# Attention values as one block product of seven instead of eight, with its sums made during the recurrent branch's output projection

## The chip, the core and the metric

The kernel runs on one core of a Trainium2 chip. Time is device microseconds of one execution on that core, the median of three runs. The profile is of one further execution, taken by the hardware profiler; its time was 864.52 us, of which 862.8 us lie between the first and the last instruction (the span).

## The reference

One layer of a hybrid encoder: 512 tokens, width 1024, float32. What the change touches is the third column block of the input projection, the values v, which the attention then weighs.

```python
xn = rmsnorm(h, norm_mix_g[l])
u = jnp.einsum('bsd,de->bse', xn, w_in[l])
q, k, v, xr, gr, ga, gb = jnp.split(u, splits, axis=-1)
ya = chunked_band_attention(q, k, v, rel_table[l]) @ w_attn_out[l]
...
yb = (hr * jax.nn.gelu(gr)) @ w_rnn_out[l]
...
# in chunked_band_attention, 16 heads of 64, chunks of 64 tokens, band of 9 chunks
p = jax.nn.softmax(s, axis=-1).astype(v.dtype)
o = jnp.einsum('bhnqk,bnkhd->bnqhd', p, vb)
```

So v is a product of 512 x 1024 tokens by 1024 x 1024 weights.

## The kernel before

All matrices are held in two parts: a high part rounded to the format fp32r and a low part, the rest. `split` (L80) makes them, the high part by a copy on ScalarE (ACT, L82), the low part by a subtraction on VectorE (DVE, L83). A product of two such values is three matmuls, high by high, high by low and low by high (`mm3`, L74; its matmuls are L76 to L78). TensorE (PE) writes them into PSUM, of which there are eight banks of 512 columns: four with the tag mm, two s, two t.

The stages in order: the normalized tokens are turned into `xnT` (feature rows by token columns, 8 blocks k of 128 features); the recurrent branch's projections (xr, gr and the gates); q and k of head pair 0; value unit 0; yb, the recurrent branch's output projection, in eight tiles of 24 matmuls, with the scores of head 0 ahead of its seventh tile; q and k of pair 1; value unit 1; the scores of head 1; then 16 heads. Each head turns its probabilities with PE (`transposed`), fills in a q or k tile of a later pair, makes the scores of the head two further on, and weighs the values (`weigh`, L973). After them ya, wo and the feed-forward layer. The latter already makes its products of weight and token blocks by seven products for eight (`block_product`).

A value unit (`v_unit`, L890) makes two of the four groups of 256 value columns (0 and 3, then 1 and 2) for all tokens: four token tiles, 8 k, three matmuls of 512 columns each, 96 in all, into four mm banks. The result is split from PSUM into v.

Weights come through a plan of chunks (`plan`, `prefetch` L311, `weights` L339): each chunk is loaded from DRAM by the SP queue into one of three raw buffers of 512 KB (tag raw), and split into one of four buffers of both parts (tag whl), one chunk ahead of the work that uses it. A raw buffer is free for the next load once it is split; a whl buffer once its last matmul has read it.

The order on each engine is set by a scheduler that lists instructions as the code's order and its own estimates have it, except in stretches under `manual_schedule`, where the named engines follow the order of the code. PE does so in the heads. Engines run their queues in order, and wait for each other by semaphores.

## Time and profile before

| what | value |
|---|---|
| time, median of 3 runs | 864.15 us (863.87 to 864.16) |
| time of the profiled execution | 864.52 us |
| its span | 862.8 us |
| PE busy | 853.1 us, 99% of the span, 4938 matmuls |
| DVE busy | 601.8 us, 70% |
| ACT busy | 497.5 us, 58% |
| POOL (GpSimd) busy | 95.9 us, 11% |
| moved by DMA | 96.38 MB, mean 112 GB/s |
| value unit 0 on PE | from 185.3 us |
| yb on PE | from 208.0 us |
| value unit 1 on PE | 262.8 to 284.6 us |

A row of a group names the line, the engine, the operation, the tile written and the tiles read, the shapes and the count; then busy time and the mean of one in ns; then how long the engine was idle just before these instructions and what ended it. A window's row has the busy time of PE, PEld (weight loads into the array), DVE, ACT and POOL, each with its count of instructions, then the granted clock of TensorE as a share, the busy share of the DMA engines and GB/s. A matmul's duration in the trace overlaps the next one's; the pace is the distance from start to start.

### The profile page before, as it was taken

The page shows a single profiled execution, that of the slowest core. Times are in us where ns is not written, and L with a number is a line of the kernel's source. Part 1 is how long each engine was busy: PE and PEld are TensorE (multiplying, and loading weights), DVE is VectorE, ACT ScalarE, POOL GpSimd, SP SyncE. Part 2 cuts the span into 40 slices and gives each one's busy share as a digit, 9 for nine tenths or more (in the row PEclk, how much of TensorE's full clock was granted, in tenths as well). Part 3 has the DMA queues.
Part 4 walks back from the last instruction along what each step waited for, and adds up shares of the span by engine and source line. Part 5 has one row for each costly group of instructions (what it writes and reads, how often), then busy time and mean ns, then how long its engine had stood idle before and what let it go on. Part 6 is the DMA issues. An engine that isn't in the chain of part 4 may idle for free.

```text
span 862.8 us, 13012 instructions
## 1 busy us (share of the span) xinstructions
PE 853.1 (99%) x4938; PEld 750.9 (87%) x4938; DVE 601.8 (70%) x950; ACT 497.5 (58%) x878; POOL 95.9 (11%) x161
## 2 busy tenths in 40 slices
PE   8999999999999999999999999999999999999997
PEld 6988888888888888888888889999999999888885
DVE  5567656664333788787556557987888888698885
ACT  6595847754123688787533357555655556545434
POOL 2412111120010233333000000000000001000000
PEclk9999999999999999999999999999999999999998
DMA  8233232433333233222233622424333332437542
GB/s 281 66 112 107 75 112 84 123 97 98 98 110 96 76 98 108 77 81 68 74 98 119 247 67 69 135 91 131 98 99 98 98 99 94 139 103 233 178 134 98
DMA packets 88895, 96.38 MB, mean 112 GB/s; under 512 B 5912, under 2 KB 75120, under 8 KB 88832
## 3 DMA queue, kind: packets, MB, share of 16 engines
q1 hardware_dynamic: 87200, 92.03, 34.7%
q10 hardware_dynamic: 1232, 2.95, 0.9%
q8 instruction: 39, 0.64, 0.3%
q0 software_dynamic: 400, 0.57, 0.2%
q14 instruction: 24, 0.20, 0.1%
HBM read 93.39 MB, written 2.14 MB: 111 GB/s over the span
## 4 chain that ended last, share of the span: by engine, by line
PE 97%; DVE 1%; ACT 1%; DMA 0%; issue 0%; ACTq 0%; DVEq 0%
PE po_out L76 2%; PE po_out L78 2%; PE po_out L77 2%; PE o L973 2%; PE p_fu L78 2%; PE p_fg L78 2%; PE p_fg L77 2%; PE p_fg L76 2%; PE p_fu L76 2%; PE p_fu L77 2%; PE pT L953 2%; PE po_gb L76 2%; PE po_xr L77 2%; PE po_xr L76 2%; PE po_ga L78 2%; PE po_k L76 2%
## 5 line engine op out<-in xcount | busy, mean ns | idle before, releaser
L942 POOL TENSOR_SCALAR p<-p,rl 128x128 f32<-128x128 f32 (+3 forms) x61 | 37.6, 636 | 91.1 <-DVE rl L938 85.9
L936 DVE CUSTOM_DVE_ANT_0 p<-s,bias 128x128 f32<-128x128 f32 (+2 forms) x64 | 28.7, 486 | 12.1 <-PE s L928 9.9
L937 ACT ACTIVATE p<-p,m 128x128 f32<-128x128 f32 (+2 forms) x64 | 35.6, 557 | 2.5 <-DVE m L936 2.2
L1158 POOL TENSOR_TENSOR act_lo<-act,act_hi 128x1024 fp32r<-128x1024 f32 x1 | 2.4, 2412 | 304.6 <-ACT act_hi L1157 304.6
L83 DVE TENSOR_TENSOR whl_qk<-raw_qk,whl_qk 128x1024 fp32r<-128x1024 f32 x16 | 20.3, 1270 | 18.5 <-ACT whl_qk L82 18.1
L76 PE MATMUL po_out<-whl_fo,act_hi 128*128 128x512 f32 (+1 forms) x80 | 30.8, 385 | 0.5 <-ACT c_u L373 0.5
L78 PE MATMUL po_out<-whl_fo,act_lo 128*128 128x512 f32 (+1 forms) x80 | 30.7, 384 | 0.0
L77 PE MATMUL po_out<-whl_fo,act_hi 128*128 128x512 f32 (+1 forms) x80 | 30.7, 384 | 0.0
L82 ACT ACTIVATE whl_qk<-raw_qk 128x1024 fp32r<-128x1024 f32 x16 | 16.9, 1055 | 20.5 <-PE po_v L78 9.8
L83 DVE TENSOR_TENSOR whl_fu_s<-s_fu,whl_fu_s 128x1024 fp32r<-128x1024 f32 x20 | 24.1, 1222 | 6.2 <-ACT whl_fu_s L82 6.2
L83 DVE TENSOR_TENSOR pp<-pT,pp 128x384 fp32r<-128x384 f32 (+1 forms) x48 | 26.9, 595 | 2.1 <-ACT pp L82 1.8
L77 PE MATMUL po_xr<-xnT,whl_xr 128*128 128x512 f32 (+1 forms) x80 | 27.7, 353 | 0.0
L77 PE MATMUL po_gr<-xnT,whl_gr 128*128 128x512 f32 (+1 forms) x80 | 27.5, 347 | 0.0
L78 PE MATMUL po_gr<-xnT,whl_gr 128*128 128x512 f32 (+1 forms) x80 | 27.3, 347 | 0.0
L78 PE MATMUL po_xr<-xnT,whl_xr 128*128 128x512 f32 (+1 forms) x80 | 27.2, 346 | 0.0
L76 PE MATMUL po_gr<-xnT,whl_gr 128*128 128x512 f32 (+1 forms) x80 | 27.1, 347 | 0.0
L83 DVE TENSOR_TENSOR whl_fg_s<-s_fg,whl_fg_s 128x1024 fp32r<-128x1024 f32 x20 | 24.0, 1223 | 4.1 <-ACT whl_fg_s L82 4.0
L76 PE MATMUL po_xr<-xnT,whl_xr 128*128 128x512 f32 (+1 forms) x80 | 26.3, 351 | 0.4 <-ACT xnT L569 0.4
L76 PE MATMUL po_k<-xnT,whl_qk 128*128 128x512 f32 x64 | 25.5, 398 | 0.0
L76 PE MATMUL po_q<-xnT,whl_qk 128*128 128x512 f32 x64 | 25.5, 398 | 0.0
L76 PE MATMUL po_ga<-xnT,whl_ga 128*128 128x512 f32 x64 | 25.4, 397 | 0.0
L76 PE MATMUL po_gb<-xnT,whl_gb 128*128 128x512 f32 x64 | 25.2, 394 | 0.0
(487 smaller groups left out, 3207.3 us busy)
## 6 DMA issues: line engine op xcount, KB each, us to landing
raw_fg<-in_w_ffn_in_dram SPq DMA_DIRECT2D x24, 512.0 KB, 4.2
raw_fu<-in_w_ffn_in_dram SPq DMA_DIRECT2D x22, 512.0 KB, 3.7
raw_qk<-in_w_in_dram SPq DMA_DIRECT2D x32, 256.0 KB, 3.1
raw_fo<-in_w_ffn_out_dram SPq DMA_DIRECT2D x16, 512.0 KB, 3.4
raw_xr<-in_w_in_dram SPq DMA_DIRECT2D x8, 512.0 KB, 3.5
raw_gr<-in_w_in_dram SPq DMA_DIRECT2D x8, 512.0 KB, 4.1
raw_ga<-in_w_in_dram SPq DMA_DIRECT2D x8, 512.0 KB, 4.1
raw_gb<-in_w_in_dram SPq DMA_DIRECT2D x8, 512.0 KB, 3.5
```

The source lines that it names most:

```text
L76: pe.matmul(o, sh, mh, start=start, stop=False, skip_group_check=parts)
L77: pe.matmul(o, sh, ml, start=False, stop=False, skip_group_check=parts)
L78: pe.matmul(o, sl, mh, start=False, stop=stop, skip_group_check=parts)
L82: act.activation(hi, src, AF.Copy)
L83: dve.tensor_sub(lo, src, f(hi))
L936: dve.tensor_tensor_reduce(prob[qb][:], scs[qb][:, 0:w], bias[:, S - w:S], -1.0, 3e38, ALU.add, ALU.min, nmax[:, qb:qb + 1])
L937: act.activation(prob[qb][:], prob[qb][:], AF.Exp, bias=nmax[:, qb:qb + 1], scale=-1.0, accum_out=lsum[:, qb:qb + 1])
L942: eng.tensor_scalar(prob[qb][:], prob[qb][:], rl[:, qb:qb + 1], 1.0, ALU.mult, ALU.mult)
L953: pe.transpose(pt[:, at * P:(at + 1) * P], prob[qb][:, kb * P:(kb + 1) * P], ident[:])
L973: pe.matmul(po[:, S - n:S], st, pp[i][:, part, lo:lo + n], start=kb == 0 and part == 0, stop=kb == NT - 1 and part == 1)
L1158: (dve if i else pool).tensor_sub(lo[:], o[:], f(hi[:]))
```

## The change

The tokens are cut into two halves of 256 and the features into two halves of 512, which gives blocks x11, x12, x21, x22 (token half, feature half); the value weights into w11, w12, w21, w22 (feature half, column side: groups 0 and 3, or 1 and 2). With

- s1 = x21 + x22, s2 = s1 - x11, s3 = x11 - x21, s4 = x12 - s2 (made by `x_sums`, each from both parts of the blocks),
- t1 = w12 - w11, t2 = w22 - t1 (`v_weight_sums`), t3 = t2 - w11, t4 = w21 - t2 (`v_weights`),

the seven products are x11 w11, s1 t1, s2 t2, s4 w22, s3 t3, x12 w21 and x22 t4. Each is two token tiles x 4 k x 3 = 24 matmuls of 512 columns. They accumulate in three pairs of banks, x and z (mm) and y (t). Copies on ACT keep an intermediate state of a bank (`keep`), adds on DVE join it with another bank, and the sums are split into v (`summed`, `given`).

The token sums s1 to s4 and the weight sums t1 and t2 are written in the code ahead of and inside yb. q and k of pair 1 go ahead of yb, and the scores of heads 0 and 1 lie inside it, ahead of its fifth and seventh tile. The seven products come after yb, directly ahead of head 0, and PE has them in the order of the code. The value weights are loaded in 14 buffers of 512 KB where there were 8: w11 comes three times, w22 twice, w12 and w21 once, each in two halves of its k, in 28 transfers of 256 KB for 16.

On PE 24 matmuls are fewer; from head 1 on the order of PE, DVE, ACT and POOL is as before. Three places where rows moved follow.

DVE during yb, from its first tile on. In the names, zb is the gate tile that is multiplied by a tile of yb out of PSUM, whl_yb the low part of yb's weights; before:

```order
L999 SCALAR_TENSOR_TENSOR zb0_456<-zb0_456,po_yb0_1858 128x512
L83 TENSOR_TENSOR whl_yb4_0_1921<-raw_yb4_0_1922,whl_yb4_0_1921 128x1024
L999 SCALAR_TENSOR_TENSOR zb0_456<-zb0_456,po_yb1_1894 128x512
L83 TENSOR_TENSOR whl_yb4_4_1926<-raw_yb4_4_1927,whl_yb4_4_1926 128x1024
L999 SCALAR_TENSOR_TENSOR zb2_457<-zb2_457,po_yb2_1920 128x512
L83 TENSOR_TENSOR whl_yb6_0_1983<-raw_yb6_0_1984,whl_yb6_0_1983 128x1024
L999 SCALAR_TENSOR_TENSOR zb2_457<-zb2_457,po_yb3_1956 128x512
L83 TENSOR_TENSOR whl_yb6_4_1988<-raw_yb6_4_1989,whl_yb6_4_1988 128x1024
L999 SCALAR_TENSOR_TENSOR zb4_458<-zb4_458,po_yb4_1982 128x512
```

and now, from the low part of s1 on (v_s1 is the buffer in which s1, s2 and s4 are made in turn, v_s1l and v_s2l are low parts, v_t1 and v_t2 the weight sums of the first half of the k blocks):

```order
L83 TENSOR_TENSOR v_s1l_1793<-v_s1_1787,v_s1h_1792 128x1024
L83 TENSOR_TENSOR whl_yb4_0_1870<-raw_yb4_0_1871,whl_yb4_0_1870 128x1024
L932 TENSOR_TENSOR v_s1_1787<-v_s1_1787,xnT_155 128x1024
L1105 SCALAR_TENSOR_TENSOR zb0_456<-zb0_456,po_yb1_1843 128x512
L83 TENSOR_TENSOR whl_yb4_4_1875<-raw_yb4_4_1876,whl_yb4_4_1875 128x1024
L934 TENSOR_TENSOR v_s1_1787<-v_s1_1787,xnT_155 128x1024
L322 TENSOR_TENSOR v_t1_0_1939<-raw_v_t_010_1933,raw_v_t_000_1930 128x1024
L1105 SCALAR_TENSOR_TENSOR zb2_457<-zb2_457,po_yb2_1869 128x512
L83 TENSOR_TENSOR v_s2l_1799<-v_s1_1787,v_s2h_1798 128x1024
L932 TENSOR_TENSOR v_s3_1788<-xnT_155 128x1024
L323 TENSOR_TENSOR v_t2_0_1940<-raw_v_t_110_1936,v_t1_0_1939 128x1024
L934 TENSOR_TENSOR v_s3_1788<-v_s3_1788,xnT_155 128x1024
```

Between the yb weights and zb rows stand token sums, weight sums and low parts.

DVE ahead of head 0. Before, the rows during value unit 1 (weights of later pairs, then the values out of PSUM):

```order
L83 TENSOR_TENSOR whl_qk2_0_2283<-raw_qk2_0_2284,whl_qk2_0_2283 128x1024
L83 TENSOR_TENSOR whl_qk2_4_2289<-raw_qk2_4_2290,whl_qk2_4_2289 128x1024
L83 TENSOR_TENSOR whl_qk3_0_2421<-raw_qk3_0_2422,whl_qk3_0_2421 128x1024
L83 TENSOR_TENSOR v1_2343<-po_v1_0_2219,v1_2343 128x2x128
L83 TENSOR_TENSOR v1_2343<-po_v1_1_2220,v1_2343 128x2x128
L83 TENSOR_TENSOR v2_0_2344<-po_v1_0_2219,v2_0_2344 128x2x128
L83 TENSOR_TENSOR v2_0_2344<-po_v1_1_2220,v2_0_2344 128x2x128
```

and now, during the products with t3 and w21:

```order
L337 TENSOR_TENSOR raw_v_t3_001_2280<-v_t2_1_2049,raw_v_t3_001_2280 128x1024
L83 TENSOR_TENSOR whl_v_t3_0_2272<-raw_v_t3_000_2274,whl_v_t3_0_2272 128x1024
L341 TENSOR_TENSOR v_t2_0_1940<-raw_v_w21_100_2323,v_t2_0_1940 128x1024
L83 TENSOR_TENSOR whl_v_t3_1_2273<-raw_v_t3_001_2280,whl_v_t3_1_2273 128x1024
L985 TENSOR_TENSOR v_keep0_2189<-v_z0_2157,v_keep0_2189 128x512
L341 TENSOR_TENSOR v_t2_1_2049<-raw_v_w21_101_2329,v_t2_1_2049 128x1024
L83 TENSOR_TENSOR whl_v_w21_0_2321<-raw_v_w21_100_2323,whl_v_w21_0_2321 128x1024
L985 TENSOR_TENSOR v_keep0_2189<-v_z1_2158,v_keep0_2189 128x512
L83 TENSOR_TENSOR v_big_2191<-v_keep0_2189,v_big_2191 128x2x128
L83 TENSOR_TENSOR v2_0_2312<-v_keep0_2189,v2_0_2312 128x2x128
L83 TENSOR_TENSOR whl_v_w21_1_2322<-raw_v_w21_101_2329,whl_v_w21_1_2322 128x1024
```

The sums of the weights stand between the low parts that they feed, and the values are split out of the kept sum in SBUF.

The SP queue ahead of head 0. Before, from the weights of value unit 1 on:

```order
L172 DMA raw_v1_0_0_2144<-in_w_in_dram 128x2x256 x2
L172 DMA raw_v1_0_2_2150<-in_w_in_dram 128x2x256 x2
L657 DMA bias2_2462<-ext_d_446 128x512
L172 DMA raw_v1_1_0_2224<-in_w_in_dram 128x2x256 x2
L172 DMA raw_v1_1_2_2230<-in_w_in_dram 128x2x256 x2
L172 DMA raw_qk2_0_2284<-in_w_in_dram 128x4x128 x2
L172 DMA raw_qk2_4_2290<-in_w_in_dram 128x4x128 x2
```

and now, from w11 on:

```order
L314 DMA raw_v_w11_000_2090<-in_w_in_dram 128x2x256 x2
L314 DMA raw_v_w11_001_2095<-in_w_in_dram 128x2x256 x2
L314 DMA raw_v_w22_110_2232<-in_w_in_dram 128x2x256 x2
L694 DMA bias3_2625<-ext_d_446 128x512
L314 DMA raw_v_w22_111_2237<-in_w_in_dram 128x2x256 x2
L314 DMA raw_v_t3_000_2274<-in_w_in_dram 128x2x256 x2
L314 DMA raw_v_t3_001_2280<-in_w_in_dram 128x2x256 x2
L314 DMA raw_v_w21_100_2323<-in_w_in_dram 128x2x256 x2
L314 DMA raw_v_w21_101_2329<-in_w_in_dram 128x2x256 x2
L169 DMA raw_qk2_0_2413<-in_w_in_dram 128x4x128 x2
L169 DMA raw_qk2_4_2419<-in_w_in_dram 128x4x128 x2
```

Each value load writes a raw buffer by two transfers (x2), and the loads of t3 and w21 stand between w22 and the weights of pair 2.

The diff, without the removed lines of `v_homes` and `v_unit`, which the listing above shows:

```diff
--- before.py
+++ after.py
@@ -109,16 +109,13 @@
 
     v_groups = ((0, 3), (1, 2))
 
-    def plan_v(u):
-        for kh in range(2):
-            plan(f"v{u}_{kh}", *(cols(w_in, C_V + gr * CW) for gr in v_groups[u]), rows=kh * S, kts=KT // 2)
-
+    v_kinds = ("w11", "t1", "t2", "w22", "t3", "w21", "t4")
     plan_qk(0)
-    plan_v(0)
+    plan_qk(1)
     for j in range(0, KT, 2):
         plan(f"yb{j}", cols(w_rnn_out, j * P))
-    plan_qk(1)
-    plan_v(1)
+    for kind in v_kinds:
+        plan(f"v_{kind}")
     for pr in range(2, HEADS // 2):
         plan_qk(pr)
     for j in (4, 6):
@@ -308,11 +305,51 @@
             return lambda part, k, at=every: hl[:, part, at]
         return lambda part, k, at=every: hl[:, part, k, at]
 
+    v_t1, v_t2 = [], []
+
+    def v_raw(kind, kh, half, u):
+        raw = wp.tile([P, 2, S], F32, tag="raw", bufs=3, name=f"raw_v_{kind}_{kh}{half}{u}")
+        at = kh * S + u * CW
+        for n, gr in enumerate(v_groups[half]):
+            sp.dma_start(out=raw[:, :, n * CW:(n + 1) * CW],
+                         in_=w_in[at:at + CW, C_V + gr * CW:C_V + (gr + 1) * CW].rearrange("(k p) e -> p k e", p=P))
+        return raw[:]
+
+    def v_weight_sums(u):
+
+        b11, b12, b22 = v_raw("t", 0, 0, u), v_raw("t", 0, 1, u), v_raw("t", 1, 1, u)
+        t1, t2 = (aw.tile([P, 2, S], F32, tag="v", bufs=4, name=f"v_t{n}_{u}")[:] for n in (1, 2))
+        dve.tensor_sub(t1, b12, b11)
+        dve.tensor_sub(t2, b22, t1)
+        v_t1.append(t1)
+        v_t2.append(t2)
+
+    def v_weights(kind):
+
+        hl = [wp.tile([P, 2, 2, S], F32R, tag="whl", bufs=4, name=f"whl_v_{kind}_{u}") for u in range(2)]
+        for u in range(2):
+            if kind == "t1":
+                src = v_t1[u]
+            elif kind in ("t2", "t4"):
+                src = v_t2[u]
+            elif kind == "t3":
+                src = v_raw(kind, 0, 0, u)
+                dve.tensor_sub(src, v_t2[u], src)
+            else:
+                src = v_raw(kind, int(kind[1]) - 1, int(kind[2]) - 1, u)
+                if kind == "w21":
+                    dve.tensor_sub(v_t2[u], src, v_t2[u])
+            split(hl[u][:, 0], hl[u][:, 1], src)
+        return lambda part, k: hl[k // 2][:, part, k % 2]
+
     def prefetch(n):
         while len(made) < min(n, len(chunks), index.get(barrier[0], len(chunks))):
             name, parts, rows, kts = chunks[len(made)]
             if name in strassen:
                 made.append(weight_sums(name))
+                continue
+            if name[:2] == "v_":
+                made.append(v_weights(name[2:]))
                 continue
             if not parts:
                 made.append(out_sums(name, rows))
@@ -468,7 +505,7 @@
     gm_p = ps.tile([P, S], F32, tag="s", bufs=2, name="gm_p")
     pe.transpose(gm_p[:, 0:8], gm_r[:], ident[0:8, 0:8])
     gm = cp.tile([P, 8], F32, name="gm")
-    _, xnT = features(xnp, "xn", "xnT")
+    xn_all, xnT = features(xnp, "xn", "xnT")
 
 
     vc = cp.tile([P, NV], F32, name="vc")
@@ -876,36 +913,101 @@
 
     vs = {}
 
...
+    def x_block(half, kh, part):
+        return xn_all[:, 4 * kh:4 * kh + 4, part, half * 256:half * 256 + 256]
+
+    def x_sums():
+
+        s, s3 = (zp.tile([P, 4, 256], F32, tag="late", bufs=2, name=f"v_s{n}")[:] for n in (1, 3))
+        out = {}
+
+        def parted(key, src):
+            pl, tag = (aw, "v") if key == "s4" else (aw2, "pt")
+            hi, lo = (pl.tile([P, 4, 256], F32R, tag=tag, bufs=4, name=f"v_{key}{n}") for n in "hl")
+            split(hi[:], lo[:], src)
+            out[key] = hi, lo
+
+        def chain(dst, first_, *rest):
+            (op, one, two) = first_
+            tc.keep_in_program_order(op(dst, one, two))
+            for op, one in rest:
+                op(dst, dst, one)
+
+        add, sub = dve.tensor_add, dve.tensor_sub
+        chain(s, (add, x_block(1, 0, 0), x_block(1, 1, 0)), (add, x_block(1, 0, 1)), (add, x_block(1, 1, 1)))
+        parted("s1", s)
+        chain(s, (sub, s, x_block(0, 0, 0)), (sub, x_block(0, 0, 1)))
+        parted("s2", s)
+        chain(s3, (sub, x_block(0, 0, 0), x_block(1, 0, 0)), (add, x_block(0, 0, 1)), (sub, x_block(1, 0, 1)))
+        chain(s, (sub, x_block(0, 1, 0), s), (add, x_block(0, 1, 1)))
+        return out, parted, s, s3
+
+    def v_pairs(gr, half):
+
         if gr in v_groups[0]:
...
+            o = aw.tile([P, 2, S], F32R, tag="v", bufs=4, name=f"v{gr}_{half}")[:]
+        elif gr == v_groups[1][0]:
+            o = v_big[0][:, half]
         else:
...
+            o = zp.tile([P, 2, S], F32R, tag="late", bufs=2, name=f"v{gr}_{half}")[:]
+        for t in range(2):
+            vs.setdefault(gr, {})[2 * half + t] = o[:, t].rearrange("p (a b d) -> p a b d", a=2, b=4)
+
+    v_big = []
+
+    def v_all(sums):
+        out, parted, s, s3 = sums
+        x_, y_ = ([mm_tile(f"v_{n}{a}", tag) for a in range(2)] for n, tag in (("x", "mm"), ("y", "t")))
+        z_ = [mm_tile(f"v_z{a}") for a in range(2)]
+
+        def product(banks, kind, rows, start):
+            w = weights(f"v_{kind}")
+            for a in range(2):
+                for k in range(4):
+                    if isinstance(rows, str):
+                        hi, lo = (o[:, k, a * P:(a + 1) * P] for o in out[rows])
+                    else:
+                        hi, lo = (x_block(*rows, part)[:, k, a * P:(a + 1) * P] for part in range(2))
+                    mm3(banks[a][:], hi, lo, w(0, k), w(1, k), start and k == 0, k == 3, parts=True)
+
+        def keep(o, banks):
+            for a in range(2):
+                act.activation(o[:, a], banks[a][:], AF.Copy)
+
+        def given(half, side, src):
+            for a in range(2):
+                for n, gr in enumerate(v_groups[side]):
+                    v = vs[gr][2 * half + a]
+                    split(v[:, :, 0::3], v[:, :, 1:3], src(a)[:, n * CW:(n + 1) * CW].rearrange("p (a b d) -> p a b d", a=2, b=2))
+
+        def summed(o, banks, half, side):
+            for a in range(2):
+                dve.tensor_add(o[:, a], banks[a][:], o[:, a])
+            for gr in v_groups[side]:
+                v_pairs(gr, half)
+            given(half, side, lambda a: o[:, a])
+
+        product(x_, "w11", (0, 0), True)
+        keeps = [rnp.tile([P, 2, 2, S], F32, tag="big", bufs=4, name=f"v_keep{n}") for n in range(2)]
+        v_big.append(rnp.tile([P, 2, 2, S], F32R, tag="big", bufs=4, name="v_big"))
+        x1, x2, z1 = keeps[0][:, 0], keeps[0][:, 1], keeps[1][:, 0]
+        keep(x1, x_)
+        product(z_, "t1", "s1", True)
+        keep(z1, z_)
+        parted("s4", s)
+        product(x_, "t2", "s2", False)
+        keep(x2, x_)
+        parted("s3", s3)
+        product(z_, "w22", "s4", False)
+        summed(x2, z_, 0, 1)
+        product(x_, "t3", "s3", False)
+        summed(z1, x_, 1, 1)
+        product(y_, "w21", (0, 1), True)
+        summed(x1, y_, 0, 0)
+        product(x_, "t4", (1, 1), False)
+        for gr in v_groups[0]:
+            v_pairs(gr, 1)
+        given(1, 0, lambda a: x_[a][:])
 
 
     def scores(h):
@@ -989,19 +1091,20 @@
             return gate(0, h - 8)
         (k_tile if h % 2 else q_tile)(2 + h // 2)
 
-    v_unit(0)
+    q_tile(1)
+    k_tile(1)
+    sums = x_sums()
     probs = {}
     for j in range(KT):
-        if j == 6:
-            probs[0] = scores(0)
+        if j in (4, 6):
+            probs[j // 2 - 2] = scores(j // 2 - 2)
         po = mm_tile(f"po_yb{j}")
         project(po, weights(f"yb{j - j % 2}"), j % 2, rnn)
+        if j in (3, 5):
+            v_weight_sums(j // 2 - 1)
         dve.scalar_tensor_tensor(zB[j], zB[j], 1.0, po[:], ALU.add, ALU.mult)
-    q_tile(1)
-    k_tile(1)
-    v_unit(1)
-    probs[1] = scores(1)
     with tc.manual_schedule(engines={mybir.EngineType.PE}):
+        v_all(sums)
         for h in range(HEADS):
             pp = transposed(h, probs.pop(h))
             fill(h)
```

More of the change, by code (lines that the diff above doesn't have):

```diff
@@ L877, in block_kernel @@
     vs = {}
-    def v_homes(gr):
+    def x_block(half, kh, part):
[21 more added lines that the diff above has]
+        return out, parted, s, s3
@@ L880, in v_homes @@
+    def v_pairs(gr, half):
         if gr in v_groups[0]:
-            return [aw.tile([P, 2, 4, HD], F32R, tag="v", bufs=8, name=f"v{gr}_{t}") for t in range(NT)]
-        if gr == v_groups[1][0]:
-            big = rnp.tile([P, 2, 2, S], F32R, tag="big", bufs=4, name=f"v{gr}")
-            rows = [big[:, t // 2, t % 2] for t in range(NT)]
-        else:
-            pairs = [zp.tile([P, 2, S], F32R, tag="late", bufs=2, name=f"v{gr}_{n}") for n in range(2)]
-            rows = [pairs[t // 2][:, t % 2] for t in range(NT)]
@@ L888, in v_homes @@
-        return [o.rearrange("p (a b d) -> p a b d", a=2, b=4) for o in rows]
-    def v_unit(u):
-        po = [mm_tile(f"po_v{u}_{t}") for t in range(NT)]
-        for kh in range(2):
-            wv = weights(f"v{u}_{kh}")
-            for kk in range(0, 4, 2):
-                for t in range(NT):
-                    toks = slice(t * P, (t + 1) * P)
-                    for k in (kk, kk + 1):
-                        xk = xnT[4 * kh + k]
-                        mm3(po[t][:], xk[:, 0, toks], xk[:, 1, toks], wv(0, k, every), wv(1, k, every),
-                            kh == k == 0, kh == 1 and k == 3)
-        homes = [v_homes(gr) for gr in v_groups[u]]
-        for t in range(NT):
-            for n, gr in enumerate(v_groups[u]):
-                v = homes[n][t]
-                v = v[:] if gr in v_groups[0] else v
-                split(v[:, :, 0::3], v[:, :, 1:3],
-                      po[t][:, n * CW:(n + 1) * CW].rearrange("p (a b d) -> p a b d", a=2, b=2))
-                vs.setdefault(gr, []).append(v)
+            o = aw.tile([P, 2, S], F32R, tag="v", bufs=4, name=f"v{gr}_{half}")[:]
+        elif gr == v_groups[1][0]:
+            o = v_big[0][:, half]
+        else:
+            o = zp.tile([P, 2, S], F32R, tag="late", bufs=2, name=f"v{gr}_{half}")[:]
```

## The prediction

> **Bound.** I read the page's first part, then the waits of PE, the windows of the stages that the change touches, PE's timeline there, and the groups of DVE and ACT by form.
>
> ```profile
> PE 853.1 (99%) x4938; PEld 750.9 (87%) x4938; DVE 601.8 (70%) x950; ACT 497.5 (58%) x878; POOL 95.9 (11%) x161
> PE busy L399 <- DVE eps_t L405: 1.2, 1, 1.2
> PE pt_mix_0t L567 <- DVE xs_mix L547: 1.1, 2, 0.9
> PE po_out L76 <- ACT c_u L373: 0.5, 1, 0.5
> PE po_xr L76 <- ACT xnT L569: 0.4, 2, 0.2
> ```
>
> PE is busy 99% of the span. Its four waits add up to 3.2 us, and they belong to the start and to the switch to the output stage. None lies in yb, the values or the attention. In the windows below the columns are PE, PEld, DVE, ACT and POOL busy, then clock, DMA share and GB/s: first value unit, yb, heads 0 to 7, and the feed-forward stage, which is already done as seven products for eight.
>
> ```profile
> 185.30:207.10 21.80, 21.80 (x98) 18.04 (x97) 9.68 (x13) 8.75 (x14) 2.94 (x3) 1.00 0.39 120
> 208.00:251.90 43.90, 43.90 (x196) 36.40 (x195) 17.10 (x27) 12.31 (x20) 2.22 (x5) 1.00 0.30 90
> 284.60:360.00 75.40, 75.40 (x422) 66.06 (x421) 60.36 (x142) 59.14 (x138) 25.51 (x46) 1.00 0.30 85
> 520.00:740.00 220.00, 220.00 (x1835) 219.91 (x1834) 180.28 (x249) 133.20 (x239) 2.41 (x1) 1.00 0.32 100
> ```
>
> PE has no gap in any of them at full granted clock, so time there is the number of matmuls times their pace. DVE is idle for 61% of yb (17.10 of 43.90). In the feed-forward stage PE stays dense with DVE at 82% (180.28 of 220), in the heads at 80%.
>
> **Removed.** Each value unit is 4 token tiles x 8 k x 3 = 96 matmuls of 512 columns, 192 for two. The pace:
>
> ```profile
> 185.32 0.39 PE L76 MATMUL po_v<-whl_v,xnT 128*128 128x512 f32 x1
> 207.08 0.22 PE L927 MATMUL s<-kh,q 128*128 128x128 f32 x1
> ...
> 208.00 0.39 PE L76 MATMUL po_yb<-rnn,whl_yb 128*128 128x512 f32 x1
> ```
>
> 96 starts lie from the first of these to the second, so (207.08 - 185.32) / 96 = 0.2267 us per matmul (the 0.39 is a duration that overlaps the next). Seven products of 2 x 4 x 3 = 24 make 168. 24 matmuls fall away: 24 x 0.2267 = 5.44 us. All other PE work remains: the q and k tiles of pair 1 and the scores of head 1 only change places. The shapes of the new matmuls are those of the old, so I take the pace to 1%: 5.39 to 5.50.
> The Trainium skill (TensorE: Matmul & The Clock Gate, back-to-back issue gap) gives 215.7 ns for 512 columns on a warm array; the trace here has 226.7, so it does not agree. By that page the gain would be 5.18 us; I stay with the row.
>
> **Added.** These rows carry the prices (busy, mean ns).
>
> ```profile
> L83 DVE TENSOR_TENSOR whl_fu_s<-s_fu,whl_fu_s 128x1024 fp32r<-128x1024 f32 x20 | 24.1, 1222 | 6.2 <-ACT whl_fu_s L82 6.2
> L386 DVE TENSOR_TENSOR c_u<-q_fu,keepa_fu 128x512 f32<-128x512 f32 x10 | 6.9, 690 | 3.5 <-PE q_fu L78 2.8 <-ACT keepa_fu L373 0.7
> L999 DVE SCALAR_TENSOR_TENSOR zb<-zb,po_yb 128x512 f32<-128x512 f32 x8 | 5.5, 688 | 12.0 <-PE po_yb L78 12.0
> L864 DVE TENSOR_TENSOR kl<-po_k,kh 64x512 fp32r<-64x512 f32 x16 | 11.0, 687 | 1.4 <-ACT kh L863 1.0
> L83 DVE TENSOR_TENSOR v<-po_v,v 128x256 fp32r<-128x256 f32 x16 | 6.4, 421 | 3.3 <-ACT v L82 3.1
> L936 DVE CUSTOM_DVE_ANT_0 p<-s,bias 128x512 f32<-128x512 f32 x16 | 10.9, 682 | 0.0
> L936 DVE CUSTOM_DVE_ANT_0 p<-s,bias 128x384 f32<-128x384 f32 x16 | 8.8, 550 | 0.2
> L936 DVE CUSTOM_DVE_ANT_0 p<-s,bias 128x256 f32<-128x256 f32 x16 | 6.7, 420 | 0.0
> L936 DVE CUSTOM_DVE_ANT_0 p<-s,bias 128x128 f32<-128x128 f32 x16 | 4.7, 292 | 11.9 <-PE s L928 9.9 <-POOL p L942 1.8
> L936 DVE DVE_READ_ACCUMULATOR2_ANT m<- 128x1 f32 x64 | 5.2, 82 | 0.0
> L938 DVE RECIPROCAL rl<-l 128x4 f32<-128x4 f32 x16 | 2.8, 174 | 1.3 <-ACT p L937 1.3
> L82 ACT ACTIVATE whl_v<-raw_v 128x1024 fp32r<-128x1024 f32 x8 | 8.4, 1055 | 9.1 <-issue 6.6 <-PE po_yb L78 1.7 <-PE po_k L78 0.8
> L82 ACT ACTIVATE v<-po_v 128x256 fp32r<-128x256 f32 x16 | 5.7, 379 | 4.0 <-DVE v L83 2.4 <-PE po_v L78 1.5
> L852 ACT ACTIVATE q<-po_q 64x512 fp32r<-64x512 f32 x16 | 9.5, 594 | 14.0 <-PE po_q L78 12.8 <-DVE q L853 0.8
> ```
>
> No row of before has the sums of the token blocks, of four blocks in 1024 elements a row; the nearest is the first, an SBUF-with-SBUF operation of that size: 1.22 us, below by nothing (one element per lane and step in every such row), above by the 1.47 quoted further down. The new copies of a product (128x512, PSUM to SBUF on ACT) stand nearest to the q row: 0.59 us.
>
> Between the two PE rows 207.08 and 208.00 lie six of a head's eight score matmuls, 0.92 us; with the two of 384 columns, 2 x 384/512 x 0.2267 = 0.34, a head's scores take 1.26. yb now lasts 8 x 24 x 0.2267 + 2 x 1.26 = 46.0 us on PE. DVE in it: 25 rows of 1.22 (10 token sums, 2 low parts of sums, 4 weight sums, 5 low parts of yb weights, 2 of w11, the sum and low part with which t3 and t1 begin) = 30.6; seven zb rows 4.8; the score rows of two heads 2 x (0.29 + 0.42 + 0.55 + 0.68 + four short ones of 0.08) = 4.5; k of pair 1 1.4; reciprocals 0.3. Sum 41.6 of 46.0, 90%.
> In the seven products DVE has 18 rows of 1.22, 6 adds of 0.69, 12 splits of 0.42 and one zb: 31.9 of 38.1, 84%. ACT has there 15 x 1.06 + 6 x 0.59 + 12 x 0.38 = 24.0 of 38.1. So all fits under PE in amount; with no cover the 16 sums and low parts in yb alone would cost 19.6 us. Whether it fits in order I walked through by these durations.
>
> Loads first. Three raw buffers of 512 KB circulate, and each load waits for the split that frees its buffer. The issue rows (KB each, median us to landing) and the spread of a value load:
>
> ```profile
> raw_v<-in_w_in_dram SPq DMA_DIRECT2D x16, 256.0 KB, 3.1
> raw_yb<-in_w_rnn_out_dram SPq DMA_DIRECT2D x8, 512.0 KB, 3.5
> x<-in_x_dram SPq DMA_DIRECT2D x4, 512.0 KB, 6.4
> DMA to landing us min/median/max: 2.8/3.1/4.7
> ```
>
> Two transfers of 256 KB per buffer: 3.7 us from freed to landed. The 14 value buffers against 8 before add 3.1 MB over some 84 us, 37 GB/s on top of 90.
>
> The walk of yb (0 = its first matmul). The first k low part of pair 1 is done by 1.5, s1 by 8.0, its low part 10.4, the next yb weights (yb4) 14.7, needed at 23.0; s2 15.9; the first weight sum, whose last buffer lands at 15.3, 17.1; t2 of it 21.4; yb6 weights 23.8 and 29.4, needed at 35.1; scores of head 0 30.1; the second pair of weight sums 31.3 and 34.6 (its load lands at 33.1); scores of head 1 37.3; w11 39.7, needed at 46.0: 6 us ahead. Then DVE waits for the first t3 load until 43.4, and the first half of t1 is ready at 45.8, needed at 51.5.
>
> The walk of the products (0 = first of w11; starts at 5.44 each; the second weight half is needed 1.36 later). A half is freed 4.08 or 5.44 into its product and refilled for the second next. t1's second half is ready at 3.2 (needed 6.8); t2 6.4 and 8.4 (10.9, 12.2); w22 11.9 and 14.9 (16.3, 17.7); the second t3 load lands 15.6; t3 18.0 and 21.0 (21.8, 23.1); w21 24.1 and 26.8 (27.2, 28.6); t4 29.5 and 32.2 (32.6, 34.0). The copies and adds that free the banks all come a product earlier than the bank is written again. The smallest distance is 1.8 us, at the second halves of w21 and t4. So no PE wait.
>
> Into the heads: Head 0's turned probabilities are done on DVE 5.6 us after the products end; before, they were done 290.2 - 285.4 = 4.8 us after the transposes began:
>
> ```profile
> 285.45 0.93 PE L953 MATMUL pT<-ident,p 128*128 128x128 f32 x7
> 288.63 1.61 DVE L83 TENSOR_TENSOR pp<-pT,pp 128x512 fp32r<-128x512 f32 x3
> 293.63 1.38 PE L973 MATMUL o<-pp,v 128*128 128x512 f32 x8
> ```
>
> There o began 8.2 us after the transposes; now the same transposes, q tile and scores lie between and make it some 8 us again, and the last value rows are done after 6.0: 2 us to spare, and from there the order is the old one. (Three rows that sum to 1.79 take 1.61 here: DVE rows overlap by some 0.09, so my walk is on the slow side.)
>
> **Sum.** Span 862.8 - 5.4 = 857.4. The profiled execution took 864.5, 1.7 around its span and 0.4 above the median of the runs, 864.15. Against the median: 864.15 - 5.44 = 858.7 us, 858.3 to 859.3 if up to half a microsecond of waits is overlooked.
>
> **Rivals.**
> First, DVE's rows are longer than taken. Not all 1024-element rows last 1.22:
>
> ```profile
> L83 DVE TENSOR_TENSOR whl_ga<-raw_ga,whl_ga 128x1024 fp32r<-128x1024 f32 x8 | 11.7, 1474 | 2.4 <-ACT whl_ga L82 2.4
> 174.35 1.64 DVE L83 TENSOR_TENSOR whl_v<-raw_v,whl_v 128x1024 fp32r<-128x1024 f32 x1
> ```
>
> At 1.47 the 25 rows of yb cost 6.3 more; 2.0 go into the wait for t3's load, 4.3 arrive at t1's second half with 3.6 to spare: 0.7 us, and the 6 us of DVE waits in the products take the rest: 859.4. Against it: the long rows lie where POOL works, and POOL has only the scaling of two heads and four copies in yb, nothing in the products after their start.
> The Trainium skill (SBUF — State Buffer, who interferes with whom) says that a DVE instruction with two SBUF inputs blocks with a GpSimd instruction that reads SBUF, and the two rows agree with it. By that rule the sums here are of the exposed kind and the case above is the one to expect in part.
> Second, and slower, the same at 1.64. All 25 + 18 rows 0.42 longer: 10.5 - 2.0 against 3.6 is 4.9 us at t1; in the products 16 x 0.42 + 3.6 - 6.4 = 3.9 against 1.8 is 2.1 more. 7.0 us of waits eat the gain: 865.7; from a mean of about 1.65 the change is slower by over 0.2%. One row in the trace of before is that long, so a mean there is unlikely.
> Third, the loads decide. At the 6.4 us of the first x loads t3's second half would be 0.8 late, w21's halves 1.9 and 1.3: 4 us, 862.7, no change. At 4.7, the longest value load, 0.2. For it: three buffers and a chain of load, sum, split; against it: DMA is busy 30% to 39%.
> That the change doesn't do what it says is excluded: the built order has 24 matmuls fewer, and PE, DVE, ACT and POOL in the old order from head 1 on.
>
> **Numbers.** Forecast 0.74 (858.7), long rows 0.10 (859.4), loads 0.09 (to 862.7), slower 0.07 (865.7). A measurement tells 0.2% (1.7 us) from no change. Faster: forecast, long rows and half of the load case, 0.88; same 0.05; slower 0.07. The range 858.0 to 861.5 leaves out the slower case and the late half of the loads.
>
> **Signs.** Right: matmuls of the products at 0.227 us from start to start; no PE wait with v_x, v_z, v_y or po_yb; DVE near 90% in yb and 84% in the products; the heads as before, 5.4 us earlier. Wrong: PE waiting for the low part of t1, w21 or t4 (DVE), for a raw_v load, or in heads 0 to 2 for pp.

## The result, and the profile after

The median is 859.06 us (858.73 to 859.59, six executions) against 864.15 (863.87 to 864.43): 5.1 us less, ratio 0.9941 with a 95% interval of 0.9928 to 0.9954. The forecast was 858.7 us in a range of 858.0 to 861.5. The profiled execution took 859.59 us, its span is 857.8.

The page's first line and the waits of PE, after:

```profile
PE 848.7 (99%) x4914; PEld 746.7 (87%) x4914; DVE 636.4 (74%) x984; ACT 511.1 (60%) x894; POOL 97.0 (11%) x161
PE busy L436 <- DVE eps_t L442: 1.2, 1, 1.2
PE po_out L76 <- ACT c_u L410: 0.5, 1, 0.5
PE po_xr L76 <- ACT xnT L606: 0.4, 2, 0.2
PE pt_mix_0t L604 <- DVE xs_mix L584: 0.2, 1, 0.2
```

24 matmuls are gone, DVE has 34.6 us more work and ACT 13.6, and PE waits where it waited before: at the start and at the switch to the output stage. No wait names v_x, v_z, v_y, po_yb or a head. The windows of yb, the seven products and heads 0 to 7 (PE, PEld, DVE, ACT, POOL busy, then clock, DMA share, GB/s):

```profile
196.40:242.30 45.90, 45.90 (x208) 38.22 (x207) 37.82 (x52) 18.64 (x31) 6.71 (x12) 1.00 0.54 172
242.50:280.60 38.10, 38.10 (x169) 31.48 (x168) 30.71 (x40) 24.50 (x36) 0.00 (x0) 1.00 0.34 101
280.60:356.00 75.40, 75.40 (x419) 66.00 (x418) 60.38 (x136) 58.24 (x133) 23.54 (x42) 1.00 0.34 96
```

DVE's share of yb rose from 39% to 82%, and PE stays dense over it. PE's timeline at both ends of the products:

```profile
242.53 0.39 PE L76 MATMUL v_x<-whl_v_w,xnT 128*128 128x512 f32 x1
...
280.39 0.39 PE L78 MATMUL v_x<-whl_v_t,xnT 128*128 128x512 f32 x1
280.62 0.49 PE L1055 MATMUL pT<-ident,p 128*128 128x128 f32 x3
```

168 matmuls in 280.62 - 242.53 = 38.09 us are 0.2267 each, the pace of before. To see where 5.09 of the expected 5.44 us went, here are three marks on PE, the first q matmul, the first weighing of head 0 and the last matmul of all, in the timeline before (its mark in the middle, 293.63, stands in the prediction):

```profile
174.44 0.39 PE L76 MATMUL po_q<-xnT,whl_qk 128*128 128x512 f32 x1
...
856.09 0.28 PE L78 MATMUL po_last<-whl_fo,act_lo 128*128 128x256 f32 x1
```

and after:

```profile
174.67 0.39 PE L76 MATMUL po_q<-xnT,whl_qk 128*128 128x512 f32 x1
...
288.47 0.62 PE L1075 MATMUL o<-pp,v 128*128 128x512 f32 x2
...
850.91 0.28 PE L78 MATMUL po_last<-whl_fo,act_lo 128*128 128x256 f32 x1
```

The touched stretch fell from 119.19 to 113.80 us, by 5.39; the rest up to the last matmul is 562.46 and 562.44. The start came 0.23 later, and what follows the last matmul took 6.89 after 6.71.

### The profile page after: what moved, and what is told of

It reads as the page before. It is cut to its first block, busy times and chain, and to the rows that moved or that the text cites. A ratio compares the mean times of both kernels' runs of the same rounds, so it can differ in the third digit from the quotient of the medians.

```text
span 857.8 us, 13023 instructions
## 1 busy us (share of the span) xinstructions
PE 848.7 (99%) x4914; PEld 746.7 (87%) x4914; DVE 636.4 (74%) x984; ACT 511.1 (60%) x894; POOL 97.0 (11%) x161
## 4 chain that ended last, share of the span: by engine, by line
PE 97%; DVE 1%; DMA 1%; ACT 1%; issue 0%; ACTq 0%; SPq 0%; DVEq 0%
PE po_out L76 2%; PE po_out L78 2%; PE po_out L77 2%; PE o L1075 2%; PE p_fu L78 2%; PE p_fg L78 2%; PE p_fg L77 2%; PE p_fg L76 2%; PE p_fu L76 2%; PE p_fu L77 2%; PE pT L1055 2%; PE po_gb L76 2%; PE po_xr L77 2%; PE po_xr L76 2%; PE po_ga L78 2%; PE po_q L76 2%
## 5 line engine op out<-in xcount | busy, mean ns | idle before, releaser
L1039 ACT ACTIVATE p<-p,m 128x128 f32<-128x128 f32 (+1 forms) x64 | 35.5, 555 | 5.3 <-DVE m L1038 5.0
L1038 DVE CUSTOM_DVE_ANT_0 p<-s,bias 128x128 f32<-128x128 f32 (+1 forms) x64 | 28.6, 486 | 11.3 <-PE s L1030 9.2
L76 PE MATMUL po_ga<-xnT,whl_ga 128*128 128x512 f32 x64 | 25.4, 397 | 0.0
L78 PE MATMUL po_ga<-xnT,whl_ga 128*128 128x512 f32 x64 | 25.0, 391 | 0.1
L77 PE MATMUL po_ga<-xnT,whl_ga 128*128 128x512 f32 x64 | 25.0, 390 | 0.0
```

The costliest lines, as they stand in the source:

```text
L76: pe.matmul(o, sh, mh, start=start, stop=False, skip_group_check=parts)
L77: pe.matmul(o, sh, ml, start=False, stop=False, skip_group_check=parts)
L78: pe.matmul(o, sl, mh, start=False, stop=stop, skip_group_check=parts)
L1038: dve.tensor_tensor_reduce(prob[qb][:], scs[qb][:, 0:w], bias[:, S - w:S], -1.0, 3e38, ALU.add, ALU.min, nmax[:, qb:qb + 1])
L1039: act.activation(prob[qb][:], prob[qb][:], AF.Exp, bias=nmax[:, qb:qb + 1], scale=-1.0, accum_out=lsum[:, qb:qb + 1])
```

## Experiments

Where no word is said of it, the listed edit leaves what is computed as it was, up to rounding.

### The changed kernel again

No edit; five executions beside the kernel before.

> The changed kernel once more, beside the kernel before, in five rounds. It is to settle whether the change is worth the 24 matmuls (5.44 us) or the 5.09 us by which the two medians differ. Theory (the pace times the count, all else hidden): the stretch from the first yb matmul to the first transpose of head 0 is again 5.4 shorter than the same work before, the median 5.2 to 5.6 below that of the kernel before, and what differs from 5.44 lies outside the touched stretch, at the start or after the last matmul. Rival (some hidden waits of 0.3 to 0.4 in the products): the same 5.1, and a PE wait of 0.3 or more between the first yb matmul and head 2.

859.22 us (859.08 to 859.39) against 864.28 (864.21 to 864.48), ratio 0.9941 (0.9929 to 0.9954): again 5.06. In its trace the first q matmul starts at 174.28 and head 0 is weighed from 288.06, so the stretch lasts 113.78, 5.41 less than before, and PE has the first three waits of the list above and no other. The rival with hidden waits falls. Nearly all of the missing 0.35 us lies outside the stretch that was changed. Between profiles of one and the same kernel the start moved by 0.39 (174.67, 174.28); which part of the 0.35 belongs to the start and which to the end stays open, since the one profile of before is of an execution that took 864.52, above its own median.

### The order alone

Against the changed kernel, shortened:

```diff
-    for kind in v_kinds:
-        plan(f"v_{kind}")
+    plan_v(0)
+    plan_v(1)
...
-    sums = x_sums()
...
-        if j in (3, 5):
-            v_weight_sums(j // 2 - 1)
...
-        v_all(sums)
+        v_unit(0)
+        v_unit(1)
```

> The new order alone: q and k of pair 1 ahead of yb, both heads' scores inside yb, the values after yb with PE in the code's order, but the values still made as eight products (the two value units of the kernel before, 192 matmuls), with no sums. Theory (the gain is the count of matmuls): the same time as the kernel before, 864.15 within 0.5 us, that is some 5.1 to 5.6 above the changed kernel. Rival (the order gives part of the gain, because it takes waits or a slow start of head 0 away): 861 to 863.5. Rival (the order costs something that the seven products hide): above 865.

864.80 us (864.66 to 864.93), ratio 1.0006 (0.9997 to 1.0014). So the order brings nothing; by the medians it costs some 0.5, though the interval also holds no difference, and from there to the changed kernel, 24 matmuls fewer, are 5.58 us. Of the 0.5, its trace shows one new wait:

```profile
PE po_v L76 <- DVE v L83: 0.2, 1, 0.2
```

With the units side by side, the second needs the four banks that the first has just filled, and at the third of them waits for the splits out of it (one matmul there starts 0.33 us later than the pace). The seven products alternate between x, z and y and have no such place.

### The cover taken away

```diff
-    sums = x_sums()               # ahead of yb
...
-        if j in (3, 5):
-            v_weight_sums(j // 2 - 1)
...
+    sums = x_sums()               # behind yb's eight tiles
+    for u in range(2):
+        v_weight_sums(u)
```

> The cover taken away: the changed kernel with its token sums and weight sums written behind yb's eight tiles, directly ahead of the seven products, instead of ahead of and inside yb. Same matmuls, same sums. Theory (16 rows of DVE that only yb hides): PE waits some 5 us at the product with t1, for the low part of s1, and some 6 us at the product with w22, for s4, since only the product with w11 and the one with t1 lie over the sums: 11 us, 870 (868 to 872). Rival (DVE has room in the products too, at 81% busy, and the place of the sums does not matter): within 1 us of the changed kernel, 859 to 860. Upper end, if nothing covers the 16 rows and their low parts: 19.6 us, 879.

877.77 us (877.34 to 878.18): 18.6 above the changed kernel and 13.5 above the one before. The places were right, the price was not. Waits of PE, and the windows right behind the first of them and behind the last (columns as above):

```profile
PE v_z L76 <- ACT v_s1h L82: 8.4, 1, 8.4
PE v_z L78 <- DVE v_s4l L83: 2.7, 1, 2.7
PE v_z L76 <- ACT v_s4h L82: 2.1, 1, 2.1
```

```profile
256.20:260.20 4.00, 3.89 (x8) 2.65 (x9) 3.67 (x3) 0.18 (x1) 0.00 (x0) 0.50 0.00 0
...
275.00:280.40 5.40, 5.39 (x13) 4.23 (x14) 4.14 (x4) 0.00 (x0) 0.00 (x0) 0.50 0.62 191
```

The waits are 13.2 us where 11 were expected: DVE, which takes its rows in order, stood 3.67 us for a load of the weight sums and 1.59 for t3's first, while the token sums queued behind them. Nearly all of the other 5 us is no wait. In both windows the granted clock is 0.50, and a matmul takes 0.427 us from start to start:

```profile
258.54 0.63 PE L77 MATMUL v_z<-whl_v_t,v_s1h 128*128 128x512 f32 x1
258.97 0.63 PE L78 MATMUL v_z<-whl_v_t,v_s1l 128*128 128x512 f32 x1
259.40 0.63 PE L76 MATMUL v_z<-whl_v_t,v_s1h 128*128 128x512 f32 x1
```

The 21 matmuls right behind the waits start 0.33 to 0.74 us apart, which is 4.8 us more than at the pace. The Trainium skill (TensorE: Matmul & The Clock Gate, the HAM clock gate) says that the array falls to half clock after an idle window of about 3.4 us and then needs as long a busy one, with 426.7 ns per matmul of 512 columns; the 0.427 here agrees. The idle time does not: in the runs below, half clock follows single gaps of 2.4 to 3.0 us as well.

### More rows in the cover

```diff
         chain(s, (sub, s, x_block(0, 0, 0)), (sub, x_block(0, 0, 1)),
+              *(n * ((add, x_block(0, 1, 0)), (sub, x_block(0, 1, 0)))))     # n = 4, 6
```

> The changed kernel with eight more DVE rows of 1024 elements in yb: the sum s2 has one token block added and subtracted four times before it is split (8 x 1.14 us from start to start = 9.1 us). It measures how much DVE work the cover still takes. Theory (DVE's idle time in yb and the first products, 8.1 us in yb's window and the waits of the products behind it, takes them, since the scheduler lets the rows of the sums s3 and s4 slide into the products, where they are needed only 16 and 22 us after the products begin): no PE wait, 859.1 to 859.5. Rival (the margins of the prediction's walk, 6 us at w11 and 3.6 at the second half of t1, are what there is): 3 to 6 us of waits at t1, 862 to 866, and above that by the slow matmuls (0.427 for 0.227 us) that followed the long PE waits of the two runs before.

> The same with twelve more rows (13.7 us). Theory (a walk through its order with 1.14 us a row): t1 and t2 still in time, but s4's low part is done some 4.3 us after the product with w22 could begin; one PE wait of 4.3 us there, then matmuls at half pace for 3.4 to 10 us as in the runs before, which adds 1.7 to 5: 865 to 869. Rival (a wait costs only itself, the slow matmuls had another cause): 863 to 864. Rival (DVE in the products has room for these too): 859.1 to 859.6.

Eight rows: 860.60 us (860.43 to 860.94), twelve: 868.52 (868.17 to 869.06). With eight, PE loses about 1 us in small pieces at the second halves of t1, t2 and w21; the idle time took all but that of 9.1 us of rows. The truth lies between the theory (859.5) and the rival (862), nearer to the theory. With twelve the place is the walked one, s4, with waits first and then eleven matmuls at half clock. The waits are 6.5 us where 4.3 were expected; that the time still lies inside the expected 865 to 869 is in part luck, since all else cost 2.8 of the 1.7 to 5 us allowed for the slow matmuls:

```profile
PE v_z L76 <- ACT v_s4h L82: 3.8, 1, 3.8
PE v_z L78 <- DVE v_s4l L83: 2.7, 1, 2.7
```

The price is no straight line: 0 us for none, 1.4 for eight rows, 9.3 for twelve.

### More rows in the products

```diff
                 if kind == "w21":
                     dve.tensor_sub(v_t2[u], src, v_t2[u])
+                    dve.tensor_add(src, src, v_t2[u])
+                    dve.tensor_sub(src, src, v_t2[u])
```

> The changed kernel with four more DVE rows in the products: each half of w21 has t2's block added and subtracted before it is split (4 x 1.14 = 4.6 us), all between the sums of t3 and the low parts of w21. Theory (a walk through its order): the low parts of w21 are done 1.5 and then 2.8 us after PE could use them, where they were 2 to 3 us ahead before; PE waits 4.3 us in two pieces for whl_v_w, the heads follow 4.3 later: 863 to 864, and up to 3 us more if two pieces of this length bring the slow matmuls. Rival (the 1.8 us of the prediction's walk were far too small a margin, DVE has 19% idle there): 859.1 to 859.6.

865.84 us, median of ten executions (863.60 to 866.72). The waits stand where they were expected, 3.3 us by the list and 4.2 from start to start:

```profile
PE v_y L77 <- DVE whl_v_w L83: 1.7, 2, 1.2
PE v_y L76 <- ACT whl_v_w L82: 1.6, 1, 1.6
...
275.20:279.30 4.10, 4.10 (x10) 3.23 (x11) 3.62 (x6) 1.78 (x5) 0.00 (x0) 0.50 0.45 128
```

and the window behind them is at half clock. This kernel shows that price by itself: one execution took 863.6 us at a mean granted clock of 0.998, 4.4 above the changed kernel, which is about the waits alone, and the other nine 865.2 to 866.7 at 0.994 to 0.996. Of the ten, one of the nine was profiled; that the fastest ran without half clock is read from its mean clock.

### POOL reads while DVE adds

```diff
+    junk = tg_.tile([P, S], F32, tag="tg", name="junk")
+    def pool_reads(j, n):
+        for i in range(n):
+            pool.tensor_add(junk[:], zB[j], zB[j - 1])
...
+        if j:
+            pool_reads(j, 4)      # after each tile of yb
+    pool_reads(7, 16)
```

> The changed kernel with 44 additions on POOL (128x512, both inputs in SBUF, into a tile that nothing reads), 28 from yb's second tile on and 16 after its eighth; the order of PE, DVE and ACT is that of the changed kernel. It measures the price of the first two rivals of the prediction: DVE rows with two SBUF inputs that lie over POOL's reads. If the rows become longer to a mean of 1.47: by the prediction's walk 0.7 us, 859.8. At 1.64 and above: by that walk 7.0 us, 866, and more by the slow matmuls after long waits. Theory now: rows over POOL work are 1.5 to 1.65, which costs DVE some 25 x 0.35 = 9 us in yb and is just taken by its idle time there, and 4 to 6 us in the products, where the waits and margins of 2 us do not take all: 859.5 to 864, with the first PE wait at a low part of t3 or w21. Rival (POOL work does not lengthen these rows): 859.2, rows at 1.22.

884.41 us (884.32 to 884.57), 25 above the changed kernel, far beyond what any of the theories gave. DVE and POOL in yb:

```profile
219.97 2.31 DVE L323 TENSOR_TENSOR v_t<-raw_v_t,v_t 128x1024 f32<-128x1024 f32 x1
222.21 2.31 DVE L934 TENSOR_TENSOR v_s<-v_s,xnT 128x1024 f32<-128x1024 f32 x1
...
219.05 8.87 POOL L1101 TENSOR_TENSOR junk<-zb,zb 128x512 f32<-128x512 f32 x4
```

Each of these DVE rows lasts 2.31 us where it lasted 1.22, and each POOL row 2.2 where one that ran alone took 1.29. They take turns: one of each in 2.23 us. PE then waited for DVE:

```profile
PE v_x L77 <- DVE whl_v_t L83: 6.1, 3, 2.8
PE s L1029 <- DVE m L1038: 3.2, 1, 3.2
PE v_y L77 <- DVE whl_v_w L83: 2.3, 1, 2.3
```

and ran at a granted clock of 0.93 and 0.91 in the two stages. Rows with one input in PSUM, zb for example, kept their 0.68. The Trainium skill (SBUF — State Buffer, who interferes with whom) has a DVE instruction with two SBUF inputs contend with a GpSimd instruction that reads SBUF, as an exclusive lock; these rows agree, and 2.31 for 1.22 is what it costs when POOL reads all the time.

The same in a small dose, on the kernel with eight extra rows:

```diff
-        chain(s3, (sub, x_block(0, 0, 0), x_block(1, 0, 0)), (add, x_block(0, 0, 1)), (sub, x_block(1, 0, 1)))
+        p_add, p_sub = pool.tensor_add, pool.tensor_sub
+        chain(s3, (p_sub, x_block(0, 0, 0), x_block(1, 0, 0)), (p_add, x_block(0, 0, 1)), (p_sub, x_block(1, 0, 1)))
```

> The kernel with the eight extra DVE rows (860.6), with the three sums of s3 made on POOL instead of DVE. POOL stands idle there, and DVE is the engine that has too much. If POOL's rows cost DVE nothing, DVE has 3 x 1.14 = 3.4 us less, the small waits at t1, t2 and w21 (1.2 us in all) go, and the time is that of the changed kernel, 859.0 to 859.4. Theory (the run with the 44 POOL additions: DVE rows with two SBUF inputs and POOL rows that read SBUF take turns): each of the three POOL rows, about 2.4 us alone, holds up a DVE row for about its own length, 5 to 7 us in all, more than the 3.4 saved: 861 to 866, and DVE's rows between 200 and 215 us at 2.2 or more.

864.06 us (863.01 to 866.36) where the kernel with those rows on DVE took 860.60: taking three rows off the loaded engine made it 3.5 us slower.

```profile
203.37 2.70 DVE L934 TENSOR_TENSOR v_s<-v_s,xnT 128x1024 f32<-128x1024 f32 x1
207.26 2.17 DVE L83 TENSOR_TENSOR v_s1l<-v_s,v_s1h 128x1024 fp32r<-128x1024 f32 x1 [1.19 <-ACT v_s1h L82]
209.34 3.41 DVE L83 TENSOR_TENSOR whl_yb<-raw_yb,whl_yb 128x1024 fp32r<-128x1024 f32 x1
...
201.74 3.25 POOL L932 TENSOR_TENSOR v_s<-xnT 128x1024 f32<-128x1024 f32 x1
205.07 6.61 POOL L934 TENSOR_TENSOR v_s<-v_s,xnT 128x1024 f32<-128x1024 f32 x2
```

The three DVE rows took 4.6 us more than 3 x 1.22, more than the 3.4 saved. The low part of t1's first half starts at 248.91 us where it started at 245.11 with s3 on DVE, and PE waits 2.5 us for the low part of t1, with half clock behind it.

### Slower loads

```diff
-        for n, gr in enumerate(v_groups[half]):
+        for n, gr in 2 * tuple(enumerate(v_groups[half])):
```

> Each value load is made twice into the same raw buffer, the second after the first, so that a load takes some 6.7 us from the freed buffer to the landing instead of 3.7 to 4.0; DVE's rows are put in a slightly other order by the scheduler for it. Theory (three raw buffers in a chain of load, sum, split; the rival of the prediction that priced 6.4 us at 4 us): PE waits for low parts of t3 and w21, 3 to 6 us in all, 862 to 865. Rival (loads are hidden with much room): 859 to 859.6. Rival (the traffic itself slows DVE or PE): PE's starts more than 0.227 us apart in the products.

870.73 us (870.58 to 871.76), 11.5 above the changed kernel, where 3 to 6 were expected:

```profile
PE v_x L76 <- ACT whl_v_w L82: 3.9, 1, 3.9
...
SPq L314 <- DMA raw_v_t<-in_w_in_dram: 21.3, 16, 3.3
...
SPq L314 <- DMA raw_v_w<-in_w_in_dram: 10.0, 8, 2.3
...
246.30:256.90 10.60, 9.37 (x20) 6.36 (x21) 7.16 (x7) 5.21 (x6) 0.15 (x1) 0.52 0.90 287
```

The wait is at w11, ahead of the places that were expected and where the prediction's walk had 6 us to spare, and 10.6 us at half clock follow. The edit did more than meant: each second transfer waits on SP's queue for the first to land, and all later loads stand behind it, so the loads came one after the other. The two SPq lines (180 to 300 us) show these waits, 31.3 us; in the changed kernel the queue waited 0.2 us for a load of its own there. So it doesn't measure a longer load alone. Pieces come nearer, which add only issues (some 0.41 us each in the changed kernel) to a load:

```diff
+        w = CW // m                                                # m = 2, 4
         for n, gr in enumerate(v_groups[half]):
+            for i in range(m):
-            sp.dma_start(out=raw[:, :, n * CW:(n + 1) * CW], in_=...)
+                sp.dma_start(out=raw[:, :, n * CW + i * w:n * CW + (i + 1) * w], in_=...)
```

> Each value load is issued in four pieces of 128 columns instead of two of 256; same bytes. SP issues one piece in some 0.41 us (the value loads' issue rows), so the last piece starts 0.8 us later and a load takes some 4.8 us from the freed buffer to the landing instead of 4.0. Theory (margins of 2.1 to 2.7 us at the second halves of t1, t3, w21 and t4 in the changed kernel): no PE wait, 859.1 to 859.4; the prediction priced 4.7 us at 0.2. Rival (the loads already decide): 0.8 us or more, 860 and above.

> The same in eight pieces of 64 columns: six more issues of 0.41 us, a load of some 6.4 us. The scheduler puts some rows of DVE in another order for it. The prediction priced this length at 4 us of waits (w21's halves and t3's second). Theory now: the loads of w11, which stand behind six loads for the weight sums on the same queue, are late first, then those of t3 and w21; 2 to 4 us of waits, and 0 to 4 us more where they add up to more than about 2.4 us in a few us of time, after which the matmuls ran at 0.427 us each in the runs before: 861 to 867. Rival (6.4 us is hidden too, and the doubled loads cost so much only because each second transfer stood in the queue until the first had landed): 859.1 to 860.

Four pieces: 858.98 us (858.87 to 859.00), no change, though DVE stood 5.01 us instead of 3.09 for t3's first load. Eight pieces: 863.69 (862.09 to 865.51), with waits first at w11:

```profile
PE v_x L76 <- ACT whl_v_w L82: 1.3, 1, 1.3
...
PE v_x L77 <- DVE whl_v_w L83: 0.8, 1, 0.8
...
225.53 8.06 SPq L316 DMA_DIRECT2D raw_v_t<-in_w_in_dram  x16
233.69 11.68 SPq L316 DMA_DIRECT2D raw_v_w<-in_w_in_dram  x23
```

The queue issues without a pause here, 39 pieces at 0.51 us each, and w11 stands behind the loads for the weight sums. So the eight pieces measure a full queue as much as a longer load. That profile is of the fastest of ten executions (862.09, granted clock 0.999, no half clock behind the waits); in the slower ones the mean clock is down to 0.995.

## Why the prediction held, step by step

**Pace times count.** Right: 0.2267 us a matmul in the products, 5.39 and 5.41 us in the touched stretch for a forecast of 5.44. The Trainium skill's figure for matmuls back to back on a warm array (TensorE: Matmul & The Clock Gate, the HAM clock gate), 215.7 ns, would have made an estimate of 5.18, and this case does not agree with it. The order by itself brought nothing: with eight products the median is 0.5 longer.

**From span to median.** This is the term that was off: 858.7 for 859.06. The prediction took 5.44 from the median of before, as if what lies around the touched stretch were fixed; there 0.35 came back, about as much as the start alone moved between two profiles of the changed kernel (0.39). The kernel with four pieces a load, with the same matmuls, gained 5.33: in its profile the first q matmul starts at 174.02, and 6.66 us follow the last matmul. So this term moves by some 0.25 between kernels with the same matmuls; why is not shown.

**DVE's load.** In the right order, too high in size: 90% of yb by the sum, 82% measured; 84% of the products, 81% measured. The durations were right (rows of 1.22), but rows that follow each other at once start 1.14 apart, which the prediction saw in one row (1.61 for three) and left as slack. In yb's window the durations of the 52 rows add up to 41.1 us, close to the 41.6 of the sum, and these overlaps take 3.2 off; in the products they add up to 33.1, which is 1.2 above the sum, and the overlaps take 2.3 off. The Trainium skill (Vector Engine (DVE) Microarchitecture Reference, measured stream behaviour on trn2) gives 1.0417 ns a column and 75 ns an instruction, an estimate of 1.14 us for 1024 columns; the rows agree.

**The walk.** Right within 1.2 us at each place. Ends in us, from the first matmul of yb (196.43) and of the products (242.53):

| done | walked | measured | needed |
|---|---|---|---|
| s1 in yb | 8.0 | 8.7 | |
| second half of yb4's weights | 14.7 | 15.1 | 23.0 |
| second pair of weight sums | 34.6 | 33.4 | |
| w11 | 39.7 | 40.7 | 46.0 |
| first half of t1 | 45.8 | 47.0 | 51.5 |
| second half of t1 | 3.2 | 4.2 | 6.8 |
| second half of t2 | 8.4 | 8.5 | 12.2 |
| second half of t3 | 21.0 | 20.5 | 23.1 |
| second half of w21 | 26.8 | 26.5 | 28.6 |
| second half of t4 | 32.2 | 31.3 | 34.0 |

Four of these rows in DVE's timeline:

```profile
242.21 1.22 DVE L83 TENSOR_TENSOR whl_v_t<-v_t,whl_v_t 128x1024 fp32r<-128x1024 f32 x1
...
245.50 1.23 DVE L83 TENSOR_TENSOR whl_v_t<-v_t,whl_v_t 128x1024 fp32r<-128x1024 f32 x1 [1.48 <-ACT whl_v_t L82]
...
267.80 1.22 DVE L83 TENSOR_TENSOR whl_v_w<-raw_v_w,whl_v_w 128x1024 fp32r<-128x1024 f32 x1
...
272.61 1.22 DVE L83 TENSOR_TENSOR whl_v_t<-v_t,whl_v_t 128x1024 fp32r<-128x1024 f32 x1
```

The smallest distance is 2.1 us, at w21, where the walk had 1.8 there and at t4. That such a distance is real is shown by the four rows more at w21, which turned it into waits.

**The heads.** Right: the turned probabilities of head 0 are done 4.5 us after the products end (5.6 walked), and head 0 is weighed 7.85 us after its transposes begin (8 walked).

**First and second rival, longer DVE rows.** They did not come, and their bound was wrong. The prediction took 1.64 as the far end because one row of before was that long; the runs show 2.31 with POOL reading all the time and up to 3.41. The trace of before had shown it already: the group whose mean of 1.47 the prediction used holds a row of 2.32 (the three numbers are the shortest, the median and the longest in ns), so a mean hid the price.

```profile
L83 DVE TENSOR_TENSOR whl_ga<-raw_ga,whl_ga x8: 1210/1318/2316, 36.1 to 395.2; 128x1024 fp32r<-128x1024 f32 x8
```

What kept the sums at 1.22 is what the prediction named: POOL is busy 6.71 us in yb and not at all in the products. Only two rows at the start of yb, beside POOL's copies of k, were longer: 1.49 for a low part of yb's weights and 1.52 for one of the sums of s1.

**Third rival, the loads.** The size came out about right: 4.7 us priced at 0.2 measured nothing, 6.4 us priced at 4 measured 2.9 to 6.3 (4.5 by the median). But the place was wrong, w11 instead of t3 and w21, since six loads for the weight sums stand ahead of it on SP's queue, and PE waited 0.2 us at w21 and not at all at t3. So the agreement in size is luck; what t3 and w21 would have cost alone is not shown, since the wait at w11 moved all that follows.

**What no price had.** Each rival's time was the sum of its waits. In the profiles, a gap of about 2.4 us or more, or two of 1.4 and 1.75 close together, cost 1 to 5 us more at half clock, so the 865.7 of the second rival, with 4.9 us of its waits at t1, would be too low.

## What to carry to other kernels

When PE is dense and the clock full, a change that removes matmuls is worth their count times the measured pace, as long as a walk through the loaded engine's order leaves every operand a margin (the smallest here was 2.1 us; the four-piece loads, whose w21 was some 0.7 us ahead, still cost nothing); the walk tells this, the busy share doesn't. Price a missed margin with the slow matmuls behind the wait, not with the wait alone. And cover made of DVE rows with two SBUF inputs holds only while POOL leaves SBUF alone: an idle POOL is not free help.

## What the runs showed of the hardware

- After a PE pause the clock can be halved for 3 to 10.6 us (granted clock 0.50, 0.427 us for 0.2267). By the distance from start to start less the pace, it followed gaps of 2.4, 2.5, 2.9, 3.0, 3.4, 4.1 and 8.6 us, and a pair of 1.4 and 1.75 with five matmuls between; it did not follow gaps of 0.7 and 1.1, nor, in the profiled execution of the eight pieces, 1.5 and 1.0.
- The same kernel can fall on either side: 863.6 us at a mean clock of 0.998, or 865.2 to 866.7 at 0.994 to 0.996, with the same extra rows.
- DVE rows of two SBUF inputs and POOL rows that read SBUF alternate: 2.23 us for one of each, 1.14 and 1.29 alone.
- A repeated transfer into one buffer holds the whole SP queue until the first has landed (31.3 us of such waits): 11.5 us for 14 loads made twice, the half clock behind the waits included.
